# A 2-D DCT kernel: preloaded Sin table, a narrower DCT matrix, float32 loads and halves shared by VectorE and ScalarE

## The chip, the cores and the metric

The kernel runs on one core of a Trainium2 chip. A core has TensorE (matmuls, results in PSUM), VectorE, ScalarE, GpSimd and SyncE, each with its own stream of instructions; they wait for one another through semaphores. The metric is the device time of one execution in microseconds, the median over several runs.

## The reference

For each of 16 images of 64x64 the reference takes the DCT of each row and then of each column:

```python
for k in range(w):            # rows; then the same over columns
    s = 0.0
    for n in range(w):
        s += x[b, i, n] * np.cos(np.pi * k * (2 * n + 1) / (2 * w))
    result[b, i, k] = s
```

With D[n, k] = cos(pi k (2n+1) / 128) this is D^T X D for each image.

## The kernel before

All 16 images are held at once: images 2g and 2g+1 stand on partitions 0 to 63 and 64 to 127, for eight groups g of 64 columns, so that x is a tile of 128 partitions by 512 columns. There is no loop over tiles; the work is one pass with these steps.

*The DCT matrix* (L36 to L94). GpSimd writes the counts k (twice 64 columns) and 2i+1; VectorE forms k(2i+1) + 192, keeps it modulo 256 and turns it into float32 (m_int L55, q_int L65, q_f L74); ScalarE takes Sin of the scaled and shifted value (L80). The modulus is taken because k(2i+1) counts in steps of a 256th of a turn. VectorE clears the two off-diagonal quadrants (L88, L89) and casts to bf16 (L92), which gives DT_2, the 128x128 block-diagonal matrix diag(D, D). In front of the first activation the compiler puts an ACT_TABLE_LOAD, which has the line of that activation.

*The load* (L104). One DMA issued by GpSimd, from float32 in DRAM to bf16 in SBUF.

*The three passes of TensorE.* One matmul with DT_2 over all 512 columns (L107), evicted by VectorE to bf16 (L110); eight transposes against an identity, four for each half of the groups, each half evicted by VectorE (L118, L119); eight matmuls with D (L126), again in halves, each evicted as float32 (L128).

*The store* (L130). One DMA of 256 KB, issued by SyncE when both halves of y_all are there.

The order of an engine's instructions is not that of the code alone: a planner lists them, and gives an engine what it takes to be ready first, the earlier in the code before the later. Each engine then works through its own list in order. Semaphore waits are put in by the framework, by tile and region.

Of the kernel before, what the change touches and what calls it, by code (L numbers as in the profile page):

```python
# [2 lines left out]

# [5 lines left out]


@with_exitstack
def kernel(
    ctx: ExitStack,
    tc: tile.TileContext,
    x: bass.AP,
    out: bass.AP,
):
    nc = tc.nc
    PI = math.pi  # L20

    batch, H, W = x.shape
    assert H == W == 64
    N = H
    P = 128
    G = batch // 2

    f32 = mybir.dt.float32
    bf16 = mybir.dt.bfloat16
    i32 = mybir.dt.int32  # L30

    const = ctx.enter_context(tc.tile_pool(name="const", bufs=1))
    psum = ctx.enter_context(tc.tile_pool(name="psum", bufs=2, space=bass.MemoryType.PSUM))


    iota_k_mod = const.tile([P, P], i32, name="iota_k_mod")  # L36
    nc.gpsimd.iota(iota_k_mod, pattern=[[0, 2], [1, N]], channel_multiplier=0, base=0)  # L37

    iota_2i1 = const.tile([P, 1], i32, name="iota_2i1")
    nc.gpsimd.iota(iota_2i1, pattern=[[0, 1]], channel_multiplier=2, base=1)  # L40

    iota_2i1_int = const.tile([P, 1], i32, name="iota_2i1_int")
    nc.vector.tensor_scalar(  # L43
        iota_2i1_int,
        in0=iota_2i1,
        scalar1=127,
        scalar2=None,
        op0=mybir.AluOpType.bitwise_and,
    )

    iota_2i1_f = const.tile([P, 1], f32, name="iota_2i1_f")
    nc.vector.tensor_copy(iota_2i1_f, iota_2i1_int)  # L52

    m_int = const.tile([P, P], i32, name="m_int")
    nc.vector.tensor_scalar(  # L55
        m_int,
        in0=iota_k_mod,
        scalar1=iota_2i1_f,
        scalar2=192.0,
        op0=mybir.AluOpType.mult,  # L60
        op1=mybir.AluOpType.add,
    )

    q_int = const.tile([P, P], i32, name="q_int")
    nc.vector.tensor_scalar(  # L65
        q_int,
        in0=m_int,
        scalar1=255,
        scalar2=None,
        op0=mybir.AluOpType.bitwise_and,  # L70
    )

    q_f = const.tile([P, P], f32, name="q_f")
    nc.vector.tensor_copy(q_f, q_int)  # L74

    bias_tile = const.tile([P, 1], f32, name="bias_tile")
    nc.gpsimd.memset(bias_tile, -PI)  # L77

    DT_2f = const.tile([P, P], f32, name="DT_2f")
    nc.scalar.activation(  # L80
        DT_2f,
        q_f,
        mybir.ActivationFunctionType.Sin,
        scale=PI / (2.0 * N),
        bias=bias_tile,
    )

    nc.vector.memset(DT_2f[0:N, N:P], 0.0)  # L88
    nc.vector.memset(DT_2f[N:P, 0:N], 0.0)  # L89

    DT_2 = const.tile([P, P], bf16, name="DT_2")
    nc.vector.tensor_copy(DT_2, DT_2f)  # L92

    DT = DT_2[0:N, 0:N]  # L94

    ident_128 = const.tile([P, P], bf16, name="ident_128")
    make_identity(nc, ident_128)


    x_all_hbm = x.rearrange("(g pb) i j -> (pb i) g j", pb=2)  # L100
    out_all_hbm = out.rearrange("(g pb) r c -> (pb r) g c", pb=2)

    x_all = const.tile([P, G, N], bf16, name="x_all")
    nc.gpsimd.dma_start(x_all, x_all_hbm)  # L104

    psum1 = psum.tile([P, G, N], f32, name="psum1", tag="pa")
    nc.tensor.matmul(psum1, DT_2, x_all, start=True, stop=True)  # L107

    t1_all = const.tile([P, G, N], bf16, name="t1_all")
    nc.vector.tensor_copy(t1_all, psum1)  # L110

    HG = G // 2
    t1T_all = const.tile([N, G, P], bf16, name="t1T_all")
    for half in range(2):
        psum2 = psum.tile([N, HG, P], bf16, name=f"psum2_{half}", tag="pb")
        for gi in range(HG):
            g = half * HG + gi
            nc.tensor.transpose(psum2[:, gi, :], t1_all[:, g, :], ident_128)  # L118
        nc.vector.tensor_copy(t1T_all[:, half * HG:(half + 1) * HG, :], psum2)  # L119

    y_all = const.tile([P, G, N], f32, name="y_all")
    for half in range(2):
        psum3 = psum.tile([P, HG, N], f32, name=f"psum3_{half}", tag="pc")
        for gi in range(HG):
            g = half * HG + gi
            nc.tensor.matmul(psum3[:, gi, :], t1T_all[:, g, :], DT,  # L126
                             start=True, stop=True)
        nc.vector.tensor_copy(y_all[:, half * HG:(half + 1) * HG, :], psum3)  # L128

    nc.sync.dma_start(out_all_hbm, y_all)  # L130


# [1 line left out]
_INS = ['x']  # L134
_OUTS = [((16, 64, 64), 'float32')]


# [23 lines left out]
```

## Time and profile before

| | us |
|---|---|
| median of 4 runs | 14.11 (14.11 to 14.12) |
| the profiled execution | 14.11 |
| its span, first to last instruction | 12.3 |
| VectorE busy | 4.3 |
| TensorE matmuls busy | 2.5 |
| GpSimd busy | 2.0 |
| ScalarE busy | 1.7 |

Times in the profile are counted from the start of the span. PE is TensorE's matmuls, PEld its weight loads, DVE VectorE, ACT ScalarE, POOL GpSimd, SP SyncE; a q behind the name is the engine's sequencer. A DMA instruction's own time is only that of issuing it; its data lands later.

### The profile page before, as it was taken

The numbers are of one execution on the slowest core, as the hardware profiler recorded it, in microseconds if no ns is written. First come the engines' busy times: TensorE is split into PE (matmuls) and PEld (weight loads), VectorE is DVE, ScalarE is ACT, GpSimd is POOL, SyncE is SP. The second block draws the span as 40 slices with busy tenths as digits, with TensorE's granted clock in tenths as the row PEclk, the third lists the DMA queues.
The fourth block names the chain that finished last, engine by engine and source line by source line (L and its number), as shares of the span: only waits on it lengthen the run. The fifth ranks groups of instructions, "written<-read, shape, count | busy, mean of one in ns | idle before, by whom it ended". The sixth has DMA issues, their size and how long they took to land.

```text
span 12.3 us, 103 instructions
## 1 busy us (share of the span) xinstructions
PE 2.5 (20%) x17; PEld 1.4 (11%) x17; DVE 4.3 (35%) x13; ACT 1.7 (14%) x2; POOL 2.0 (16%) x10
## 2 busy tenths in 40 slices
PE   0000000000000000089003999789000000000000
PEld 0000000000000000030003993634000000000000
DVE  0001888991000006800794019989950000000000
ACT  0000000005999990000000000000000000000000
POOL 2429799980000000000000000000000000000000
DMA  0000000000899910000000000000000029990000
GB/s 0 0 0 0 0 0 0 0 0 0 54 125 151 85 11 0 0 0 0 0 0 0 0 0 0 0 0 0 0 0 0 0 50 286 289 226 1 0 0 0
DMA packets 2080, 0.39 MB, mean 32 GB/s; under 512 B 2080, under 2 KB 2080, under 8 KB 2080
## 3 DMA queue, kind: packets, MB, share of 16 engines
q0 software_dynamic: 1040, 0.13, 16.7%
q1 hardware_dynamic: 1040, 0.26, 9.4%
HBM read 0.26 MB, written 0.26 MB: 43 GB/s over the span
## 4 chain that ended last, share of the span: by engine, by line
DVE 32%; PE 14%; ACT 10%; issue 6%; ACTq 4%; POOL 3%; POOLq 0%
ACT L80 10%; DVE y_all L128 7%; DVE t_all L110 6%; PE psum L118 5%; PE psum L107 5%; DVE q_int L65 4%; DVE t1T_all L119 3%; ACTq L156 3%; PE psum L126 3%; DVE q_f L74 3%; DVE m_int L55 3%; DVE DT L92 2%; POOL iota_k_mod L37 2%; DVE iota_2i_f L52 1%; DVE iota_2i_int L43 1%
## 5 line engine op out<-in xcount | busy, mean ns | idle before, releaser
L80 ACT ACT_TABLE_LOAD x1 | 1.3, 1283 | 2.9 <-DVE q_f L74 2.9
L107 PE MATMUL psum<-x_all,DT 128*128 128x512 bf16 x1 | 0.6, 606 | 5.3 <-DVE DT L92 5.3
L118 PE MATMUL psum<-ident,t_all 128*64 128x128 bf16 x8 | 1.1, 314 | 0.8 <-DVE t_all L110 0.8
L119 DVE COPY t1T_all<-psum 64x512 bf16<-64x512 bf16 x2 | 0.8, 417 | 0.7 <-PE psum L118 0.7
L104 POOL DMA_DIRECT2D x_all<-in_x_dram x1 | 1.0, 1002 | 0.1
L118 PEld LDWEIGHTS <-t_all 128*64 128x64 bf16 x8 | 0.8, 168 | 1.3 <-DVE t_all L110 1.3
L110 DVE CAST t_all<-psum 128x512 bf16<-128x512 f32 x1 | 0.7, 692 | 0.7 <-PE psum L107 0.7
L128 DVE COPY y_all<-psum 128x256 f32<-128x256 f32 x2 | 0.9, 426 | 0.1
L126 PE MATMUL psum<-DT,t1T_all 64*128 64x64 bf16 x8 | 0.8, 236 | 0.1
L88 DVE MEMSET DT_2f<- 64x64 f32 x1 | 0.1, 112 | 1.8 <-ACT DT_2f L80 1.8
L107 PEld LDWEIGHTS <-DT 128*128 128x128 bf16 x1 | 0.1, 102 | 5.3 <-DVE DT L92 5.3
L43 DVE TENSOR_SCALAR iota_2i_int<-iota_2i 128x1 int32<-128x1 int32 x1 | 0.2, 154 | 1.2 <-POOL bias_tile L77 1.2
L65 DVE TENSOR_SCALAR q_int<-m_int 128x128 int32<-128x128 int32 x1 | 0.5, 521 | 0.0
L126 PEld LDWEIGHTS <-t1T_all 64*128 64x128 bf16 x8 | 0.5, 118 | 0.5 <-DVE t1T_all L119 0.5
L80 ACT ACTIVATE DT_2f<-q_f,bias_tile 128x128 f32<-128x128 f32 x1 | 0.4, 401 | 0.0
L74 DVE CAST q_f<-q_int 128x128 f32<-128x128 int32 x1 | 0.3, 346 | 0.0
L55 DVE TENSOR_SCALAR m_int<-iota_k_mod,iota_2i_f 128x128 int32<-128x128 int32 x1 | 0.3, 319 | 0.0
masks.py:199 POOL TENSOR_SCALAR_AFFINE_SELECT ident<-ident 128x128 bf16<-128x128 bf16 x1 | 0.3, 306 | 0.0
L37 POOL IOTA iota_k_mod<- 128x128 int32 x1 | 0.2, 236 | 0.4 <-POOLq L145 0.4
L92 DVE CAST DT<-DT_2f 128x128 bf16<-128x128 f32 x1 | 0.2, 227 | 0.0
masks.py:197 POOL MEMSET ident<- 128x128 bf16 x1 | 0.2, 201 | 0.0
L52 DVE CAST iota_2i_f<-iota_2i_int 128x1 f32<-128x1 int32 x1 | 0.2, 153 | 0.0
(7 smaller groups left out, 0.7 us busy)
## 6 DMA issues: line engine op xcount, KB each, us to landing
out_dram<-y_all SPq DMA_DIRECT2D x1, 256.0 KB, 2.4
x_all<-in_x_dram POOLq DMA_DIRECT2D x1, 128.0 KB, 3.4
```

The source lines that it names most:

```text
L37: nc.gpsimd.iota(iota_k_mod, pattern=[[0, 2], [1, N]], channel_multiplier=0, base=0)
L55: nc.vector.tensor_scalar(m_int, in0=iota_k_mod, scalar1=iota_2i1_f, scalar2=192.0, op0=mybir.AluOpType.mult, op1=mybir.AluOpType.add,)
L65: nc.vector.tensor_scalar(q_int, in0=m_int, scalar1=255, scalar2=None, op0=mybir.AluOpType.bitwise_and,)
L74: nc.vector.tensor_copy(q_f, q_int)
L80: nc.scalar.activation(DT_2f, q_f, mybir.ActivationFunctionType.Sin, scale=PI / (2.0 * N), bias=bias_tile,)
L104: nc.gpsimd.dma_start(x_all, x_all_hbm)
L107: nc.tensor.matmul(psum1, DT_2, x_all, start=True, stop=True)
L110: nc.vector.tensor_copy(t1_all, psum1)
L118: nc.tensor.transpose(psum2[:, gi, :], t1_all[:, g, :], ident_128)
L119: nc.vector.tensor_copy(t1T_all[:, half * HG:(half + 1) * HG, :], psum2)
L126: nc.tensor.matmul(psum3[:, gi, :], t1T_all[:, g, :], DT, start=True, stop=True)
L128: nc.vector.tensor_copy(y_all[:, half * HG:(half + 1) * HG, :], psum3)
```

## The change

The constants: a dummy activation of Sin on one column is put ahead of everything else; the argument table has 64 columns instead of 128; the count 2i+1 is written separately for the lower and the upper 64 partitions, so that the AND with 127 falls away; Sin writes bf16 at once; the zeroed quadrants and the cast are gone, and DT_wide holds D on partitions 0 to 63 (DT_a) and again on 64 to 127 (DT_b).

The load: two float32 loads, of groups 0 to 3 by SyncE and of groups 4 to 7 by ScalarE, into tiles of their own, and two casts to bf16 on VectorE, which `issue_after` places behind q_f in VectorE's list. A tile of 128 bytes a partition, which nothing uses, is allocated ahead of the two.

The passes: the first matmul becomes four, for each half of the groups one on the lower and one on the upper 64 partitions. Evictions of the first and third pass go to VectorE for half 0 and to ScalarE for half 1; those of the transposes stay on VectorE. The store is issued in halves, by SyncE and by ScalarE.

```diff
@@ -33,101 +33,99 @@
     psum = ctx.enter_context(tc.tile_pool(name="psum", bufs=2, space=bass.MemoryType.PSUM))
 
 
-    iota_k_mod = const.tile([P, P], i32, name="iota_k_mod")
-    nc.gpsimd.iota(iota_k_mod, pattern=[[0, 2], [1, N]], channel_multiplier=0, base=0)
+    dummy = const.tile([P, 1], f32, name="dummy")
+    nc.gpsimd.memset(dummy, 0.0)
+    nc.scalar.activation(dummy, dummy, mybir.ActivationFunctionType.Sin)
 
-    iota_2i1 = const.tile([P, 1], i32, name="iota_2i1")
-    nc.gpsimd.iota(iota_2i1, pattern=[[0, 1]], channel_multiplier=2, base=1)
+    iota_k = const.tile([P, N], i32, name="iota_k")
+    nc.gpsimd.iota(iota_k, pattern=[[1, N]], channel_multiplier=0, base=0)
 
-    iota_2i1_int = const.tile([P, 1], i32, name="iota_2i1_int")
+    iota_2i1m = const.tile([P, 1], i32, name="iota_2i1m")
+    nc.gpsimd.iota(iota_2i1m[0:N, :], pattern=[[0, 1]],
+                   channel_multiplier=2, base=1)
+    nc.gpsimd.iota(iota_2i1m[N:P, :], pattern=[[0, 1]],
+                   channel_multiplier=2, base=1)
+
+    iota_2i1f = const.tile([P, 1], f32, name="iota_2i1f")
+    nc.vector.tensor_copy(iota_2i1f, iota_2i1m)
+
+    m_int = const.tile([P, N], i32, name="m_int")
     nc.vector.tensor_scalar(
-        iota_2i1_int,
-        in0=iota_2i1,
-        scalar1=127,
-        scalar2=None,
+        m_int, in0=iota_k, scalar1=iota_2i1f, scalar2=192.0,
+        op0=mybir.AluOpType.mult, op1=mybir.AluOpType.add,
+    )
+
+    q_int = const.tile([P, N], i32, name="q_int")
+    nc.vector.tensor_scalar(
+        q_int, in0=m_int, scalar1=255, scalar2=None,
         op0=mybir.AluOpType.bitwise_and,
     )
 
-    iota_2i1_f = const.tile([P, 1], f32, name="iota_2i1_f")
-    nc.vector.tensor_copy(iota_2i1_f, iota_2i1_int)
-
-    m_int = const.tile([P, P], i32, name="m_int")
-    nc.vector.tensor_scalar(
-        m_int,
-        in0=iota_k_mod,
-        scalar1=iota_2i1_f,
-        scalar2=192.0,
-        op0=mybir.AluOpType.mult,
-        op1=mybir.AluOpType.add,
-    )
-
-    q_int = const.tile([P, P], i32, name="q_int")
-    nc.vector.tensor_scalar(
-        q_int,
-        in0=m_int,
-        scalar1=255,
-        scalar2=None,
-        op0=mybir.AluOpType.bitwise_and,
-    )
-
-    q_f = const.tile([P, P], f32, name="q_f")
-    nc.vector.tensor_copy(q_f, q_int)
+    q_f = const.tile([P, N], f32, name="q_f")
+    index_done = nc.vector.tensor_copy(q_f, q_int)
 
     bias_tile = const.tile([P, 1], f32, name="bias_tile")
     nc.gpsimd.memset(bias_tile, -PI)
 
-    DT_2f = const.tile([P, P], f32, name="DT_2f")
+    DT_wide = const.tile([P, N], bf16, name="DT_wide")
     nc.scalar.activation(
-        DT_2f,
-        q_f,
-        mybir.ActivationFunctionType.Sin,
-        scale=PI / (2.0 * N),
-        bias=bias_tile,
+        DT_wide, q_f, mybir.ActivationFunctionType.Sin,
+        scale=PI / (2.0 * N), bias=bias_tile,
     )
 
-    nc.vector.memset(DT_2f[0:N, N:P], 0.0)
-    nc.vector.memset(DT_2f[N:P, 0:N], 0.0)
-
-    DT_2 = const.tile([P, P], bf16, name="DT_2")
-    nc.vector.tensor_copy(DT_2, DT_2f)
-
-    DT = DT_2[0:N, 0:N]
+    DT_a = DT_wide[0:N, :]
+    DT_b = DT_wide[N:P, :]
 
     ident_128 = const.tile([P, P], bf16, name="ident_128")
     make_identity(nc, ident_128)
 
-
+    HG = G // 2
     x_all_hbm = x.rearrange("(g pb) i j -> (pb i) g j", pb=2)
     out_all_hbm = out.rearrange("(g pb) r c -> (pb r) g c", pb=2)
 
+    pad = const.tile([P, 32], f32, name="pad")   # 128 bytes, never used
+    x_all_f0 = const.tile([P, HG, N], f32, name="x_all_f0")
+    x_all_f1 = const.tile([P, HG, N], f32, name="x_all_f1")
+    nc.sync.dma_start(x_all_f0, x_all_hbm[:, 0:HG, :])
+    nc.scalar.dma_start(x_all_f1, x_all_hbm[:, HG:G, :])
+
     x_all = const.tile([P, G, N], bf16, name="x_all")
-    nc.gpsimd.dma_start(x_all, x_all_hbm)
-
-    psum1 = psum.tile([P, G, N], f32, name="psum1", tag="pa")
-    nc.tensor.matmul(psum1, DT_2, x_all, start=True, stop=True)
+    with tc.issue_after(index_done.ins):
+        nc.vector.tensor_copy(x_all[:, 0:HG, :], x_all_f0)
+        nc.vector.tensor_copy(x_all[:, HG:G, :], x_all_f1)
 
     t1_all = const.tile([P, G, N], bf16, name="t1_all")
-    nc.vector.tensor_copy(t1_all, psum1)
+    t1T_all = const.tile([N, G, P], bf16, name="t1T_all")
+    y_all = const.tile([P, G, N], f32, name="y_all")
+    out_engines = [nc.sync, nc.scalar]
 
-    HG = G // 2
-    t1T_all = const.tile([N, G, P], bf16, name="t1T_all")
+    def evict(half, out_, in_):
+        # VectorE takes half 0, ScalarE half 1
+        if half == 0:
+            nc.vector.tensor_copy(out_, in_)
+        else:
+            nc.scalar.copy(out_, in_)
+
     for half in range(2):
+        hs = slice(half * HG, (half + 1) * HG)
+        psum1 = psum.tile([P, HG, N], f32, name=f"psum1_{half}", tag="pa")
+        nc.tensor.matmul(psum1[0:N, :, :], DT_a, x_all[0:N, hs, :], start=True, stop=True)
+        nc.tensor.matmul(psum1[N:P, :, :], DT_b, x_all[N:P, hs, :], start=True, stop=True)
+        evict(half, t1_all[:, hs, :], psum1)
+    for half in range(2):
+        hs = slice(half * HG, (half + 1) * HG)
         psum2 = psum.tile([N, HG, P], bf16, name=f"psum2_{half}", tag="pb")
         for gi in range(HG):
-            g = half * HG + gi
-            nc.tensor.transpose(psum2[:, gi, :], t1_all[:, g, :], ident_128)
-        nc.vector.tensor_copy(t1T_all[:, half * HG:(half + 1) * HG, :], psum2)
-
-    y_all = const.tile([P, G, N], f32, name="y_all")
+            nc.tensor.transpose(psum2[:, gi, :], t1_all[:, half * HG + gi, :], ident_128)
+        nc.vector.tensor_copy(t1T_all[:, hs, :], psum2)
     for half in range(2):
+        hs = slice(half * HG, (half + 1) * HG)
         psum3 = psum.tile([P, HG, N], f32, name=f"psum3_{half}", tag="pc")
         for gi in range(HG):
-            g = half * HG + gi
-            nc.tensor.matmul(psum3[:, gi, :], t1T_all[:, g, :], DT,
+            nc.tensor.matmul(psum3[:, gi, :], t1T_all[:, half * HG + gi, :], DT_a,
                              start=True, stop=True)
-        nc.vector.tensor_copy(y_all[:, half * HG:(half + 1) * HG, :], psum3)
-
-    nc.sync.dma_start(out_all_hbm, y_all)
+        evict(half, y_all[:, hs, :], psum3)
+        out_engines[half].dma_start(out_all_hbm[:, hs, :], y_all[:, hs, :])
 
 
 # ---- launch: one core; inputs and outputs as the reference has them ----
```

## Rows read from the trace of the kernel before

**Rows 1.** The page's first part: the span, and busy time, share and instructions of each engine.

```profile
span 12.3 us, 103 instructions
PE 2.5 (20%) x17; PEld 1.4 (11%) x17; DVE 4.3 (35%) x13; ACT 1.7 (14%) x2; POOL 2.0 (16%) x10
```

**Rows 2.** The chain of waits, in order of time: start us, us, what.

```profile
0.75 0.01 POOLq L37
...
2.48 0.36 DVE q_f L74
...
2.91 1.28 ACT L80
4.19 0.42 ACTq L156
...
4.67 0.11 DVE DT_2f L88
...
4.98 0.24 DVE DT L92
...
5.27 0.62 PE psum L107
...
5.91 0.70 DVE t_all L110
...
6.66 0.65 PE psum L118 x4
...
7.33 0.43 DVE t1T_all L119
...
7.80 0.41 PE psum L126 x4
...
8.23 0.85 DVE y_all L128 x2
```

**Rows 3.** DMA issues: line, KB each, us from issue to landing.

```profile
out_dram<-y_all SPq DMA_DIRECT2D x1, 256.0 KB, 2.4
x_all<-in_x_dram POOLq DMA_DIRECT2D x1, 128.0 KB, 3.4
```

**Rows 4.** The timeline of GpSimd: start us, us, instruction [idle before].

```profile
1.03 0.13 POOL L40 IOTA iota_2i<- 128x1 int32 x1
1.10 0.10 POOL L77 MEMSET bias_tile<- 128x1 f32 x1
...
1.42 1.00 POOL L104 DMA_DIRECT2D x_all<-in_x_dram  x1
2.43 0.31 POOL masks.py:199 TENSOR_SCALAR_AFFINE_SELECT ident<-ident 128x128 bf16<-128x128 bf16 x1
```

**Rows 5.** Groups of instructions by form: line, shapes, count | busy us, mean ns | idle before.

```profile
L118 PE MATMUL psum<-ident,t_all 128*64 128x128 bf16 x8 | 1.1, 314 | 0.8 <-DVE t_all L110 0.8
L128 DVE COPY y_all<-psum 128x256 f32<-128x256 f32 x2 | 0.9, 426 | 0.1
L107 PE MATMUL psum<-x_all,DT 128*128 128x512 bf16 x1 | 0.6, 606 | 5.3 <-DVE DT L92 5.3
L65 DVE TENSOR_SCALAR q_int<-m_int 128x128 int32<-128x128 int32 x1 | 0.5, 521 | 0.0
L80 ACT ACTIVATE DT_2f<-q_f,bias_tile 128x128 f32<-128x128 f32 x1 | 0.4, 401 | 0.0
L55 DVE TENSOR_SCALAR m_int<-iota_k_mod,iota_2i_f 128x128 int32<-128x128 int32 x1 | 0.3, 319 | 0.0
L92 DVE CAST DT<-DT_2f 128x128 bf16<-128x128 f32 x1 | 0.2, 227 | 0.0
L52 DVE CAST iota_2i_f<-iota_2i_int 128x1 f32<-128x1 int32 x1 | 0.2, 153 | 0.0
```

**Rows 6.** The timeline of the transposes and of SyncE's store: start us, us, instruction.

```profile
6.66 1.06 PE L118 MATMUL psum<-ident,t_all 128*64 128x128 bf16 x8 [0.78 <-DVE t_all L110]
...
9.11 0.40 SPq L130 DMA_DIRECT2D out_dram<-y_all  x1
```

**Rows 7.** Stretches of the span: busy time of each engine, PEclk, DMA share, GB/s.

```profile
3.20:4.60 1.40, 0.00 (x0) 0.00 (x0) 0.00 (x0) 1.39 (x2) 0.00 (x0) 1.00 1.44 92
...
10.10:11.15 1.05, 0.00 (x0) 0.00 (x0) 0.00 (x0) 0.00 (x0) 0.00 (x0) 1.00 1.08 245
```

More of the change, by code (lines that the diff above doesn't have):

```diff
@@ L6 @@
 import concourse.tile as tile
-from concourse import bass_utils, mybir
+from concourse import mybir
 from concourse.masks import make_identity
```

## The prediction, made before the changed kernel had run

> **What bounds the kernel now.** I read the totals first [rows 1]: no engine is busy for more than 35% of the 12.3 us span, so nothing is limited by throughput; the kernel is one chain of hand-overs, and only what lies on that chain has a price. So the chain of waits comes next [rows 2]. The reader is to see three stretches in it. From 0.75 to 5.22 us the DCT matrix is built: GpSimd counts, VectorE makes an argument table (the last of it is q_f, done at 2.84), ScalarE loads its Sin table for 1.28 us and evaluates Sin until 4.6, VectorE clears two quadrants and casts. From 5.27 to 9.08 us the data passes through TensorE and the evictions of PSUM. From 9.11 the output is stored: 2.4 us to landing [rows 3], then 0.8 us of closing barriers to the span's end at 12.3. The profiled execution took 14.11 us, which is also the median of the four runs shown; 1.8 us of it lie outside the span, and I leave these 1.8 and the 0.8 as they are.
>
> What is not on the chain is x: its load is issued by GpSimd at 1.42 [rows 4] and takes 3.4 us to landing [rows 3], so it is there at 4.8, 0.4 us ahead of the DCT matrix. That 0.4 is the first thing to see: shortening the matrix alone would win no more than 0.4 us, so the new load counts as much as the table.
>
> **The change, part by part**, in us from the span's start.
>
> *Matrix.* The DCT argument table becomes 64 columns wide instead of 128, one of the four small VectorE steps goes (the AND on iota_2i1), and so do the two MEMSETs and the cast behind Sin (4.67 to 5.22). GpSimd does a tiny memset more ahead of its iota and one more short iota; rows of this size follow each other by some 0.07 us [rows 4], and the iota of 64 columns is shorter, so the index column is ready at about 1.25 where it was at 1.16. Then four VectorE steps: one at 128x1 took 0.153, those at 128x128 from 0.32 to 0.52 beside a working GpSimd and the plain cast 0.227 [rows 5]; at 64 columns I take 0.22 with the hand-over each, at most 0.35. q_f is done at 2.1 (2.6 at most).
>
> *Table load.* The first activation is now a dummy that depends only on a memset, so the 1.283 us load no longer waits for q_f. ScalarE also issues half of the load of x. On GpSimd the load of x ran ahead of the affine select that stands before it in the code and was not ready [rows 4], so this planner issues what is ready first; I expect the same on ScalarE, at the body's start at 0.75, with 0.40 us for the issue, as SP's row has it [rows 6]. Then the table load 1.15 to 2.43, the dummy to at most 2.83 and Sin to at most 3.23, each put at the 0.401 that the 128-wide Sin took [rows 5]. The matrix is ready by 3.25 without any step of VectorE behind it.
>
> The Trainium skill speaks against this price ("ScalarE: Activation LUTs", What ACT_TABLE_LOAD costs): each switch of table is put at some 1.28 us of load and 1.38 us of drain, 2.66 in all. Here the load begins at 2.91 and the row behind it, where Sin runs, at 4.19 [rows 2], so this trace shows nothing between them and does not agree with the page. By the page's figure the matrix would come 1.38 later, at 4.6 instead of 3.25; what that would do is rival 4.
>
> *Load of x.* One GpSimd load with a cast in flight becomes two float32 loads of 128 KB, issued by SP and ScalarE at about 0.75, with two casts on VectorE. The bytes into SBUF double to 256 KB. The nearest row is the store: 256 KB in the same 256-byte pieces, issued by SP, 2.4 us to landing; it moved 245 GB/s in the 1.05 us in which it ran fully [rows 7]. I take 2.4 for both halves together, since both run on the same DMA engines: landing at 3.15. The bounds are 1.9 (half the bytes) and 3.4, the row of GpSimd's load [rows 3]. The price of a cast: 0.153 at one column and 0.227 at 128 give 0.30 at 256 [rows 5]; 0.43 if it runs at the pace of the 256-column eviction. Cast 0 runs from 3.2 to 3.5, cast 1 from 3.53 to 3.83. So x is now what the first matmul waits for, by a quarter of a us: 3.55 instead of 5.27, a gain of 1.72. What hides the matrix is x; if x came half a us earlier, only 0.25 of it would be won.
>
> *First matmul.* One of 128 rows and 512 columns becomes two pairs of 64 rows and 256 columns. The one took 0.606 [rows 5]; eight transposes of 128 columns, 0.314 each, take 1.06 together [rows 5, 6], so they begin 0.106 apart, so a column costs 0.83 ns and 0.18 is fixed. A pair in series costs the same 0.61 and ends at 4.16; the second pair follows at once to 4.59. The eviction of half 0 takes 0.43 on VectorE, as y_all's rows at the same shape: 4.20 to 4.63. Before, matmul and eviction filled 5.27 to 6.61, that is 1.34; now 1.08: a gain of 0.26.
>
> *ScalarE's copies.* The trace has no PSUM copy on ScalarE. The nearest rows: 0.401 for its 128-wide Sin, 0.426 for VectorE's copy of this shape [rows 5]. I take 0.43, with 0.40 and 0.80 (twice the Sin's columns at twice its time) as the ends. Half 1 is evicted from 4.63 to 5.06, while the transposes of half 0 run (4.68 to 5.33, four in 0.65 as before [rows 2]), so 0.27 of slack covers it; at 0.80 the last 0.1 would show.
>
> *From there* the order is as before: copies of t1T to 5.78 and 6.21 (0.43 each), matmuls of half 1 from 6.26 to 6.67, then y half 1, now on ScalarE, to 7.12, issue at 7.15. VectorE finishes y half 0 at 6.68 and SP issues it at 6.71. From the first transpose to the last issue the trace has 2.45 (6.66 to 9.11) and my sum 2.47: ScalarE's second copy only stands where VectorE's stood, since the matmuls of half 1 end just when VectorE would be free. ScalarE at 0.80 would cost 0.37 here, with nothing to hide it.
>
> *Store.* Half 0 goes out 0.44 earlier, so its packets are almost through when half 1's start. A store of 256 KB spends about 1.06 of its 2.4 in packets [rows 7]; half of the bytes leave 1.87: landing at 9.02 instead of 11.5, of which 0.53 is the gain of the split. If two queues cost as much as one whole store, that 0.53 is gone.
>
> Sum: 1.72 + 0.26 − 0.02 + 0.53 = 2.49; 14.11 − 2.49 = 11.62, told as **11.6 us**.
>
> **The rivals.**
>
> 1. *The pair of matmuls runs side by side*: they use different rows and columns of the array, so the second need not wait for the first's columns. For it: different partitions on both sides; against: every row here shows matmuls in a queue, one after another. A pair then costs 0.18 + 0.21 = 0.39 in place of 0.61: 11.4 us. The Trainium skill has this rule ("TensorEngine Tiling (Array Packing)", Key Properties): tiles of the array work independently of each other. No run here shows it yet.
>
> 2. *ScalarE's load goes behind Sin.* If the planner keeps the code's order, half 1 of x is issued at 3.23 and lands at 5.1 (1.87 later, as half of a store). Cast 1 stands on VectorE ahead of the eviction of half 0, and half 1's matmuls on TensorE ahead of all transposes, so both halves wait: cast to 5.45, matmuls to 6.1, transposes from 6.1 instead of 4.68: 1.42 later, 13.0 us. Against it: GpSimd's order [rows 4].
>
> 3. *The dummy doesn't move the table load*: it is loaded behind q_f still, or a second time for Copy ahead of Sin. Then the load runs from 2.12 to 3.40, the matrix is ready at 3.8, 0.3 behind x: 11.9 us.
>
> 4. *ScalarE stands still behind the early load*, for about as long as the load itself takes, 1.28: the dummy begins at 3.71 and not at 2.43, the matrix is ready at 4.53, the first matmul begins at 4.58, 1.03 later: 12.65 us. The chain speaks against it: 4.19 follows 2.91 by the load's 1.28 and nothing more [rows 2]. The drain that the Trainium skill states on the page named above is this case.
>
> 5. *Slower than before.* No row shows a DMA from ScalarE. The queue of waiters in rival 2 has a point from which it decides: half 1 of x may land at 3.8 for nothing, and beyond that each us late is a us of the whole, because VectorE and TensorE work in order; from 6.3 on the kernel is slower than 14.11. That needs the issue behind Sin (3.23) and a landing as slow as GpSimd's 3.4: 6.63, which gives 14.4 us. For it: only that ScalarE's queue is unmeasured. Against it: both halves of the condition.
>
> **How the numbers follow.** My forecast 0.59, rival 1 0.23, rival 2 0.06, rival 3 0.05, rival 4 0.03, rival 5 0.03, and 0.01 that gains and losses cancel. The forecast alone with its unknown prices: ScalarE's copies (+0.5 at worst), the load (−0.25, where the matrix takes over, to +0.3, where its packets run for the 1.4 of GpSimd's load [rows 7]), casts (+0.13): 11.3 to 12.2. Rival 1 reaches below that, to 11.0 if x also comes early and the dummy and Sin are shorter than 0.4. The range is 11.0 to 12.2, which takes in rival 3 and leaves out rivals 2, 4 and 5. Faster by over 0.2% (0.03 us, about what can be told from no change): all but rival 5 and the cancelling case, 0.96; the same 0.01; slower 0.03.
>
> **What would show it.** The table load should begin before 1.2 and no second one appear; the two loads be issued before 0.9 and land near 3.15; the first matmul wait for VectorE's cast and not for Sin; two matmuls of a pair begin 0.21 apart (together, in rival 1); ScalarE's copies take about 0.43; the last issue stand near 7.15 and its landing under 1.9 behind it. I am wrong if the first matmul waits for ScalarE, if half 1 of x is issued behind Sin, or if the last landing is still 2.4 behind its issue.

## The result, and the profile after

The changed kernel takes 11.36 us in the median of 11 runs (11.23 to 11.55); the kernel before took 14.11 in 15 runs (14.10 to 14.12). The ratio is 0.799, with a 95% interval from 0.797 to 0.801. The forecast was 11.6 in a range from 11.0 to 12.2. This ratio and those below are of the fast runs alone, those within 1.5% of the fastest of their kernel, while the medians are of all runs (11.36 to 14.11 is 0.805). The profiled execution took 11.50 us with a span of 9.72, and times worked out from its trace are to be compared with 11.50.

The page's first part for the changed kernel:

```profile
span 9.7 us, 114 instructions
## 1 busy us (share of the span) xinstructions
PE 2.5 (26%) x20; PEld 1.7 (17%) x20; DVE 3.1 (31%) x10; ACT 2.5 (25%) x5; POOL 1.2 (13%) x11
```

No engine is near its limit here either. TensorE is as busy as before [rows 1]; VectorE has lost 1.2 us, and ScalarE has gained 0.8. The chain of waits (start us, us, what) shows where the time is now:

```profile
0.74 2.52 DMA x_all_f<-in_x_dram
...
3.28 0.30 DVE x_all L94
...
3.62 0.37 PE psum L112
3.99 0.07 PE psum L113
...
4.08 0.43 DVE t_all L105
...
4.56 0.65 PE psum L119 x4
...
5.23 0.43 DVE t1T_all L120
...
5.70 0.39 PE psum L125 x4
...
6.13 0.41 PE psum L125 x4
...
6.56 0.37 ACT y_all L107
```

Read it against the chain of before [rows 2]. The whole first stretch, with q_f, the table load, Sin, MEMSETs and a cast, has left the chain; one DMA and one cast stand in its place, and the first matmul begins at 3.62 instead of 5.27. The matrix is not on the chain at all. The timeline of ScalarE and TensorE (start us, us, instruction, idle before) says how early it is:

```profile
1.27 1.28 ACT L38 ACT_TABLE_LOAD   x1 [1.27 <-PEq L143]
...
2.56 0.20 ACT L38 ACTIVATE dummy<-dummy 128x1 f32<-128x1 f32 x1
2.67 0.33 ACT L71 ACTIVATE DT_wide<-q_f,bias_tile 128x64 bf16<-128x64 f32 x1
3.05 0.12 PEld L112 LDWEIGHTS <-DT_wide 64*64 64x64 bf16 x1 [3.05 <-ACT DT_wide L71]
...
3.62 0.37 PE L112 MATMUL psum<-x_all,DT_wide 64*64 64x256 bf16 x1 [3.62 <-DVE x_all L94]
...
3.63 0.42 PE L113 MATMUL psum<-x_all,DT_wide 64*64 64x256 bf16 x1
...
4.35 0.37 ACT L107 CAST t_all<-psum 128x256 bf16<-128x256 f32 x1 [1.35 <-PE psum L113]
```

The weights are loaded at 3.05, and the matmul waits 0.57 longer, for the cast of x. The two matmuls of the pair begin together. The DMA issues (KB each, us from issue to landing):

```profile
x_all_f<-in_x_dram SPq DMA_DIRECT2D x1, 128.0 KB, 2.5
x_all_f<-in_x_dram ACTq DMA_DIRECT2D x1, 128.0 KB, 2.8
out_dram<-y_all SPq DMA_DIRECT2D x1, 128.0 KB, 1.9
out_dram<-y_all ACTq DMA_DIRECT2D x1, 128.0 KB, 2.0
```

The last issue stands at 6.96, before at 9.11 [rows 6], and the last landing at 8.92 instead of 11.46.

### The profile page after: what moved, and what is told of

It is laid out like the page before. It is cut to its first block, busy times and chain, and to the rows that moved or that the text cites. A ratio compares the mean times of both kernels' runs of the same rounds, so it can differ in the third digit from the quotient of the medians.

```text
span 9.7 us, 114 instructions
## 1 busy us (share of the span) xinstructions
PE 2.5 (26%) x20; PEld 1.7 (17%) x20; DVE 3.1 (31%) x10; ACT 2.5 (25%) x5; POOL 1.2 (13%) x11
## 4 chain that ended last, share of the span: by engine, by line
DMA 26%; PE 19%; DVE 12%; ACT 4%; issue 3%
DMA x_all_f<-in_x_dram 26%; PE psum L125 8%; PE psum L119 7%; DVE t_all L105 4%; DVE t1T_all L120 4%; ACT y_all L107 4%; PE psum L112 4%; DVE x_all L94 3%; PE psum L113 1%
## 5 line engine op out<-in xcount | busy, mean ns | idle before, releaser
L112 PE MATMUL psum<-x_all,DT_wide 64*64 64x256 bf16 x2 | 0.6, 368 | 3.6 <-DVE x_all L94 3.6
L125 PE MATMUL psum<-DT_wide,t1T_all 64*128 64x64 bf16 x8 | 0.8, 236 | 0.1
L113 PE MATMUL psum<-x_all,DT_wide 64*64 64x256 bf16 x2 | 0.7, 418 | 0.0
L94 DVE CAST x_all<-x_all_f 128x256 bf16<-128x256 f32 x1 | 0.3, 293 | 1.0 <-DMA x_all_f<-in_x_dram 1.0
L105 DVE COPY y_all<-psum 128x256 f32<-128x256 f32 x1 | 0.4, 426 | 0.1
L95 DVE CAST x_all<-x_all_f 128x256 bf16<-128x256 f32 x1 | 0.3, 295 | 0.0
```

What stands on the lines that cost most here:

```text
L94: nc.vector.tensor_copy(x_all[:, 0:HG, :], x_all_f0)
L95: nc.vector.tensor_copy(x_all[:, HG:G, :], x_all_f1)
L105: nc.vector.tensor_copy(out_, in_)
L112: nc.tensor.matmul(psum1[0:N, :, :], DT_a, x_all[0:N, hs, :], start=True, stop=True)
L113: nc.tensor.matmul(psum1[N:P, :, :], DT_b, x_all[N:P, hs, :], start=True, stop=True)
L125: nc.tensor.matmul(psum3[:, gi, :], t1T_all[:, half * HG + gi, :], DT_a, start=True, stop=True)
```

## The experiments

Twelve kernels were run, each beside the kernel before (14.11 or 14.12 every time), but in three groups on different chips and not beside the changed kernel. A difference of medians from the changed kernel is therefore weaker than one of stretches in two traces.

| run | median us (lowest to highest) | ratio to before, 95% |
|---|---|---|
| table_only | 14.07 (13.98 to 14.20) | 0.993 to 0.999 |
| load_only | 13.58 (13.58 to 13.59) | 0.960 to 0.964 |
| load_behind_sin | 13.14 (13.01 to 13.16) | 0.924 to 0.934 |
| loads_on_sp | 11.58 (11.40 to 11.91) | 0.806 to 0.815 |
| gpsimd_dma_added | 14.10 (14.09 to 14.11) | 0.998 to 1.000 |
| no_dummy | 12.17 (12.15 to 12.44) | 0.860 to 0.864 |
| same_rows | 11.59 (11.42 to 11.69) | 0.809 to 0.816 |
| no_cast | 11.37 (11.22 to 11.46) | 0.794 to 0.806 |
| no_pad | 11.97 (11.88 to 11.99) | 0.844 to 0.849 |
| table_only_aligned | 13.83 (13.73 to 13.93) | 0.975 to 0.985 |
| one_store | 12.03 (12.00 to 12.07) | 0.851 to 0.854 |
| sp_loads_no_cast | 11.22 (11.05 to 11.60) | 0.785 to 0.790 |

**One part of the change alone: table_only and load_only.** The first is the kernel before plus

```diff
+    dummy = const.tile([P, 1], f32, name="dummy")
+    nc.gpsimd.memset(dummy, 0.0)
+    nc.scalar.activation(dummy, dummy, mybir.ActivationFunctionType.Sin)
```

> The kernel before with the dummy activation alone. My theory (matrix and load of x are two parallel paths that end 0.4 us apart): the matrix is ready near 4.0, but x still lands at 4.8, so the first matmul starts at 4.85 instead of 5.27 and the time is 13.7 us. Rival (one chain, each part worth its own length): the whole 1.28 us of the table load is won, 12.8 us.

Measured: 14.07. The matrix was ready at 4.0, as expected, and the first matmul waited for x until 4.98, 0.29 earlier than before. In the chain of waits:

```profile
1.43 3.51 DMA x_all<-in_x_dram
...
4.98 0.60 PE psum L111
```

But the store took 2.61 us from issue to landing instead of 2.35, and gave 0.26 of it back. Both theories missed that; it is taken up below. The DMA issue:

```profile
out_dram<-y_all SPq DMA_DIRECT2D x1, 256.0 KB, 2.6
```

The second kernel of this pair is the kernel before with

```diff
 ...
+    nc.sync.dma_start(x_all_f0, x_all_hbm[:, 0:HG, :])
+    nc.scalar.dma_start(x_all_f1, x_all_hbm[:, HG:G, :])
 ...
-    nc.gpsimd.dma_start(x_all, x_all_hbm)
+    with tc.issue_after(index_done.ins):
+        nc.vector.tensor_copy(x_all[:, 0:HG, :], x_all_f0)
+        nc.vector.tensor_copy(x_all[:, HG:G, :], x_all_f1)
```

> The kernel before with the two float32 loads and the two casts alone; the table load still stands behind q_f. My theory: x is in bf16 by 3.9, the matrix still comes at 5.22, and VectorE has the casts done before Sin ends, so the time stays 14.1 us (within 0.1). Rival (the load is what the change lives on): 12.5 us or less.

Measured: 13.58, so my theory fell: a load that was off the chain was worth 0.53. The matrix itself came earlier, and with it the first matmul, at 4.82 instead of 5.27. To see whether GpSimd's issuing of the load had slowed VectorE, that issue was put back into load_only, with a destination that nothing reads:

```diff
+    x_unused = const.tile([P, G, N], bf16, name="x_unused")
+    nc.gpsimd.dma_start(x_unused, x_all_hbm)
```

> The load-only kernel (e2) with GpSimd issuing its old load again, into a tile that nothing reads. The load-only kernel was 0.53 us faster than the kernel before although the table load stayed where it was; in its trace the AND (q_int) took 0.23 us where it took 0.52, the cast q_f 0.23 for 0.35, and q_f was done at 2.37 for 2.84. Theory A (GpSimd's 1.0 us of issuing slows the VectorE instructions beside it): q_int goes back to 0.5, q_f ends near 2.85, the time back to 14.0 to 14.1 us. Theory B (the load itself came off the path): VectorE's steps stay at 0.23 and the time at 13.6 us.

Measured: 14.10, theory A. The groups by form (busy us, mean ns) of load_only:

```profile
L55 DVE TENSOR_SCALAR m_int<-iota_k_mod,iota_2i_f 128x128 int32<-128x128 int32 x1 | 0.3, 288 | 0.0
...
L65 DVE TENSOR_SCALAR q_int<-m_int 128x128 int32<-128x128 int32 x1 | 0.2, 227 | 0.0
L74 DVE CAST q_f<-q_int 128x128 f32<-128x128 int32 x1 | 0.2, 227 | 0.0
```

and with GpSimd's DMA added:

```profile
L65 DVE TENSOR_SCALAR q_int<-m_int 128x128 int32<-128x128 int32 x1 | 0.5, 522 | 0.0
...
L74 DVE CAST q_f<-q_int 128x128 f32<-128x128 int32 x1 | 0.3, 347 | 0.0
...
L55 DVE TENSOR_SCALAR m_int<-iota_k_mod,iota_2i_f 128x128 int32<-128x128 int32 x1 | 0.3, 306 | 0.0
```

The same instruction takes 227 ns with GpSimd idle and 522 beside its DMA issue, and q_f ends at 2.82 instead of 2.37. The load's traffic is not the cause, for its packets begin at 3.1 only, behind q_f. So the old load cost nothing by its landing and 0.45 us by the engine that issued it. It does not slow every step alike: m_int, beside the same issue, took 306 ns instead of 288, and q_f's 347 fall beside the affine select, which the issue had pushed back from 1.40 to 2.42. The Trainium skill ("SBUF — State Buffer", Who interferes with whom) has a port pair that GpSimd shares with VectorE's copies, casts and tensor_scalars when these run in a fast mode; the later one waits. That q_int, begun behind the issue, lost 295 ns agrees with that in direction; no run here shows the port itself, and a wait to the issue's end at 2.40 would have put q_int's end at 2.63, where it stands at 2.43.

**The start address of a tile: no_pad and table_only_aligned.** In table_only and, further below, in no_dummy the store was slow. In both, a small tile had come or gone ahead of y_all in the partition. No trace gives a tile's address: the offsets here are counted from the tiles' sizes in order of allocation, a small tile taken as 32 bytes.

```diff
-    pad = const.tile([P, 32], f32, name="pad")   # 128 bytes, never used
```

> The changed kernel without the unused tile of 128 bytes. Two runs so far had a store slower than all others: table_only (packets 1.30 us for 256 KB, elsewhere 1.05) and no_dummy (0.75 for 128 KB, elsewhere 0.59). In both, a tile put in or left out ahead of y_all made it start 32 and 224 bytes past a multiple of 256 bytes of a partition; in all the others it starts on one. Without the unused tile it starts 128 bytes past. Theory A (a 256-byte row that straddles such a multiple costs more): packets of a half 0.75, last landing 2.2 behind its issue instead of 1.95, the loads slower as well, 11.6 to 11.9 us. Theory B (the unused tile does nothing): 11.36.

Measured: 11.97, 0.61 above the changed kernel and somewhat above theory A's range. The store's stretch (us, busy time by engine, PEclk, DMA share, GB/s) of the changed kernel:

```profile
7.50:8.60 1.10, 0.00 (x0) 0.00 (x0) 0.00 (x0) 0.00 (x0) 0.00 (x0) 1.00 1.06 238
```

and without the unused tile:

```profile
7.65:9.00 1.35, 0.00 (x0) 0.00 (x0) 0.00 (x0) 0.00 (x0) 0.00 (x0) 1.00 0.87 194
```

The same 256 KB take a quarter longer, and the last half of the store lands 2.19 behind its issue instead of 1.95. The unused tile in the change is therefore no ornament. But these 0.24 are all that the trace puts down to it. Of the 0.41 between the profiled executions (11.91 and 11.50) the other 0.17 comes with x: half 0 lands at 3.42 instead of 3.25, and with aligned tiles it landed anywhere from 3.17 (same_rows) to 3.46 (no_cast). That the loads are slower as well, as theory A has it, is therefore not shown. The Trainium skill ("DMA: Bandwidth & Descriptors", How a descriptor splits into AXI transactions) says that a descriptor which does not start on a 256-byte boundary is split into more transactions, the first of them from the boundary below; the store agrees with that in direction. Then the same repair for table_only:

```diff
+    pad = const.tile([P, 56], f32, name="pad")   # 224 bytes, never used
```

> table_only with an unused tile of 224 bytes ahead of x_all, so that x_all and y_all start on multiples of 256 bytes again. Theory A (table_only lost its gain to the store's start): the store takes 2.35 from issue to landing instead of 2.61, the load lands at 4.8 to 4.9, the first matmul starts at 4.85 to 4.95, 13.7 to 13.8 us. Theory B (the gain was lost elsewhere): 14.05 us as before.

Measured: 13.83 (13.73 to 13.93), against 14.07: theory A. The store's stretch in table_only, 256 KB at 201 GB/s:

```profile
9.75:11.05 1.30, 0.00 (x0) 0.00 (x0) 0.00 (x0) 0.00 (x0) 0.00 (x0) 1.00 0.76 201
```

and aligned:

```profile
9.70:10.75 1.05, 0.00 (x0) 0.00 (x0) 0.00 (x0) 0.00 (x0) 0.00 (x0) 1.00 1.10 249
```

**The dummy taken away: no_dummy.** The three lines of the first diff are left out of the changed kernel.

> The changed kernel without the dummy activation, so that the table load waits for q_f: rival 3 made real. My theory (matrix and x are parallel paths, x the later by some 0.5 us): q_f at 2.25, table load to 3.55, Sin to 3.9, first matmul at 4.0 instead of 3.62: 0.4 us slower than the changed kernel, 11.75 us. Rival (the dummy is worth its whole table load): 12.6 us. Rival (x hides it all): 11.36.

Measured: 12.17. On TensorE the theory held: the first matmul begins at 3.99, expected at 4.0, and its wait has changed its name, in the timeline,

```profile
3.99 0.42 PE L108 MATMUL psum<-x_all,DT_wide 64*64 64x256 bf16 x1 [3.99 <-ACT DT_wide L67]
```

and the last issue is 0.37 later. Against the profiled execution of the changed kernel the whole is 0.66 longer (12.16 and 11.50); 0.26 more of it is the store: without the dummy's 32 bytes y_all starts 224 past a multiple of 256, and the last half lands 2.21 behind its issue instead of 1.95.

**A late half: load_behind_sin and loads_on_sp.**

```diff
 ...
+    with tc.issue_after(sin_done.ins):
         nc.scalar.dma_start(x_all_f1, x_all_hbm[:, HG:G, :])
```

> The changed kernel with ScalarE's half of the load placed behind Sin in ScalarE's list: rival 2 of the prediction made real. By that rival's words both halves wait for the late one, and the time is 13.0 us less what the measured kernel is under the forecast, 12.8. But the planner's list for this kernel puts all of half 0's transposes and last matmuls ahead of half 1's first matmul and the second cast behind the copy of t1T, so I expect: half 0 as early as a load alone allows (first matmul at 3.0), half 1 one pass later, last issue near 8.2 instead of 6.96: 12.6 us. If a late half cost nothing: 11.4.

Measured: 13.14. The planner did reorder, as its timeline shows: half 1's cast (L96) and first matmul stand behind half 0's transposes.

```profile
3.41 0.37 PE L113 MATMUL psum<-x_all,DT_wide 64*64 64x256 bf16 x1 [3.41 <-DVE x_all L95]
...
5.36 0.28 DVE L96 CAST x_all<-x_all_f 128x256 bf16<-128x256 f32 x1
...
5.82 0.42 PE L113 MATMUL psum<-x_all,DT_wide 64*64 64x256 bf16 x1
```

So rival 2 had the time nearly right (13.0), by luck, and the way wrong: half 1 was there at 4.52 and waited for engines, because the planner had put it last. Most of what my 12.6 lacked is half 0's landing, 3.04 instead of 2.65. The next run asks what half 0 gains if half 1 does not share its time:

```diff
-    nc.scalar.dma_start(x_all_f1, x_all_hbm[:, HG:G, :])
+    nc.sync.dma_start(x_all_f1, x_all_hbm[:, HG:G, :])
```

> The changed kernel with both halves of the load issued by SP, half 0 first. My theory (the two queues share the same DMA engines, and packets of both halves interleave, so that half 0 lands as late as both): half 0 lands near 2.65 instead of 3.25, ScalarE's table load starts 0.5 earlier, the matrix is ready at 2.7, the first matmul starts at 3.0 instead of 3.62, half 1 lands by 3.3 and is covered by half 0's work: 10.75 us. Rival (issuing costs more than sharing: half 1 issued 0.43 later makes all 0.4 later): 11.7 us. Third: the issuer does not matter, 11.3 to 11.4.

Measured: 11.58 (11.40 to 11.91), not 10.75. Half 0, now ahead of half 1 in one queue, lands 2.29 behind its issue, not 1.9, and half 1 at 3.88, 2.66 behind its own. The timeline of VectorE, TensorE and ScalarE:

```profile
3.40 0.37 PE L112 MATMUL psum<-x_all,DT_wide 64*64 64x256 bf16 x1 [3.40 <-DVE x_all L94]
...
3.91 0.29 DVE L95 CAST x_all<-x_all_f 128x256 bf16<-128x256 f32 x1 [0.56 <-DMA x_all_f<-in_x_dram]
4.12 0.42 DVE L105 CAST t_all<-psum 128x256 bf16<-128x256 f32 x1
4.25 0.37 PE L112 MATMUL psum<-x_all,DT_wide 64*64 64x256 bf16 x1 [0.44 <-DVE x_all L95]
...
4.71 0.37 ACT L107 CAST t_all<-psum 128x256 bf16<-128x256 f32 x1 [2.02 <-PE psum L113]
```

The first matmul is 0.22 earlier and its result ready by 3.83, but VectorE stands in front of the second cast until 3.88, with the eviction behind it: it begins at 4.12 instead of 4.08. This is the queue of waiters of rivals 2 and 5; it costs half 0 some 0.25. Yet it is not what set the time. The chain that ended last runs from half 1's landing through its cast, its matmuls at 4.25 and ScalarE's eviction at 4.71 (4.35 in the changed kernel) to its transposes, and the last issue stands at 7.11 instead of 6.96.

**The pair of matmuls: same_rows.**

```diff
-        nc.tensor.matmul(psum1[N:P, :, :], DT_b, x_all[N:P, hs, :], start=True, stop=True)
+        nc.tensor.matmul(psum1[N:P, :, :], DT_a, x_all[0:N, hs, :], start=True, stop=True)
```

> The changed kernel with the second matmul of each pair reading the lower 64 partitions too (the second half of the images is left out of the result): same columns and same work, but both matmuls on the same rows of the array. Theory A (a pair runs side by side only where both its rows and its columns differ): the second begins 0.21 behind the first, the pair takes 0.61 instead of 0.42, the time 11.55 us. Theory B (different columns are enough): they still begin together, 11.36 us.

Measured: 11.59 (11.42 to 11.69), which overlaps the changed kernel's spread and decides nothing; the trace does, for theory B:

```profile
3.54 0.37 PE L112 MATMUL psum<-x_all,DT_wide 64*64 64x256 bf16 x1 [3.54 <-DVE x_all L94]
...
3.54 0.42 PE L113 MATMUL psum<-x_all,DT_wide 64*64 64x256 bf16 x1
```

The two begin together on the same rows of the array too, and VectorE's eviction of the pair begins 0.46 behind them in both kernels (4.00 after 3.54, 4.08 after 3.62). Different columns are enough.

**The casts: no_cast and sp_loads_no_cast.**

```diff
-        nc.vector.tensor_copy(x_all[:, 0:HG, :], x_all_f0)
-        nc.vector.tensor_copy(x_all[:, HG:G, :], x_all_f1)
+    x_hi = [t.bitcast(bf16).rearrange("p g (n two) -> p g n two", two=2)
+            for t in (x_all_f0, x_all_f1)]
 ...
```

> The changed kernel without the two casts: TensorE reads the upper 16 bits of each float32 of x as bf16, every second element of the tile, so x is cut to bf16 instead of rounded. My theory (x's landing and cast set the first matmul): it begins right behind the landing, at 3.3 instead of 3.62, and the time is 11.03 us. Rival (reading every second element slows the matmul): the pair takes 0.85 instead of 0.42 and eats the gain, 11.4 us or more. Rival (the matrix takes over): first matmul at 3.1 or later in any case, so at most 0.5 is won.

Measured: 11.37 (11.22 to 11.46): no gain in the median. The matmul runs at its old pace (0.37 and 0.42) and begins 0.04 behind the landing, but in this execution the landing came at 3.46; fifteen of the sixteen parts of the load were there by 3.16. Why the fastest of the four executions was not below 11.22 either is open, and so is what the casts are worth.

The next run joins these edits to that of loads_on_sp:

```diff
-    nc.scalar.dma_start(x_all_f1, x_all_hbm[:, HG:G, :])
+    nc.sync.dma_start(x_all_f1, x_all_hbm[:, HG:G, :])
 ...
```

> Both loads on SP, half 0 first (as loads_on_sp), and no casts (as no_cast, x cut to bf16). In loads_on_sp half 0 was ready 0.2 earlier, but VectorE stood behind the late half's cast, so the eviction of half 0 began no earlier; without casts this wait is gone. Theory A: first matmul at 3.07, eviction of half 0 by 3.95, half 1 lands at 3.6 to 3.9, transposes of half 0 from 4.1 to 4.35 instead of 4.56, 10.9 to 11.15 us. Theory B (a late half 1 holds TensorE, whose half-1 matmuls stand ahead of the transposes): transposes not before 4.4, 11.25 us or more.

Measured: 11.22 (11.05 to 11.60), between the theories. Transposes begin at 4.25, the time of theory A, but by the way of theory B: half 0's eviction ends at 3.99, and half 1's matmuls, which stand ahead on TensorE, hold the transposes back. Half 1 lands at 3.85 and now leads the chain,

```profile
1.22 2.63 DMA x_all_f<-in_x_dram
...
3.90 0.37 PE psum L110
```

with a wait of its eviction between the two halves of the transposes. The kernel's interval against before (0.785 to 0.790) is below that of the changed kernel (0.797 to 0.801), about 1% faster. But the two were not run beside each other, their spreads overlap, and x is cut instead of rounded.

**The split of the store: one_store.**

```diff
-        out_engines[half].dma_start(out_all_hbm[:, hs, :], y_all[:, hs, :])
+    nc.sync.dma_start(out_all_hbm, y_all)
```

> The changed kernel with one store of 256 KB on SP behind both halves of y. My theory (half 0's packets run while half 1 is still computed): issued at 6.96 it lands 2.35 later instead of 1.95, so 0.4 us slower than the changed kernel, 11.75 us; the prediction had put this term at 0.53. Rival (two stores share the DMA engines and cost as much as one): 11.36.

Measured: 12.03. From the last issue to the landing the single store takes 2.33, the second half of the split one 1.95: 0.38 of the 0.40 expected. The DMA issue:

```profile
out_dram<-y_all SPq DMA_DIRECT2D x1, 256.0 KB, 2.3
```

In the profiled executions (12.00 and 11.50) another 0.09 is a later first matmul, at 3.71. The medians differ by 0.67. The four executions of one_store lie within 12.00 to 12.07, so x presumably came late in all of them; why it did is open.

## Why the forecast came out as it did

*What bounds the kernel, and what follows the table load: right.* Matrix and x are two paths, and x became the later one. The first matmul began at 3.62, forecast 3.55. The two paths miss each other by 0.57, where I had 0.3: the table load began 0.12 late, behind an issue of ScalarE of 0.49 instead of 0.40, but the dummy took 0.20 and Sin 0.33 instead of 0.4 each. That shortening the matrix alone wins at most 0.4 held: 0.28 with aligned tiles. That it is the load that must come along held as well, though load_only showed a second reason, which the prediction did not have: the load's issue on GpSimd had lengthened the matrix's own path by 0.45.

*Load of x: the size was off.* From the store I took 1.9 for one half and 2.4 for both; a half alone lands 2.30 behind its issue (load_behind_sin), both at 2.52 and 2.78. That half 1 came 0.37 behind the forecast, at 3.52 instead of 3.15, cost nothing by luck: its cast stands behind half 0's on VectorE and began at 3.55, forecast 3.53. The cast took 0.29, as worked out.

*First matmul: the step that failed.* "A pair in series" was the likeliest case; the pair runs side by side, rival 1. From first matmul to first transpose it is 0.94 where I had 1.13. Before it was 1.39; no run separates what the pair and what the halving gave of that step. The Trainium skill's rule that stood beside rival 1 ("TensorEngine Tiling (Array Packing)", Key Properties) agrees with the trace.

*ScalarE's copies*: 0.372, not 0.43, and below the bound of 0.40 that I had put under them. From first transpose to last issue 2.40, forecast 2.47.

*Store*: the last half lands 1.95 behind its issue, forecast 1.87.

*No stand-still behind the table load* (rival 4): the dummy begins at 2.56, the load ends at 2.55. The drain of 1.38 us that the Trainium skill states ("ScalarE: Activation LUTs", What ACT_TABLE_LOAD costs) is not there in this kernel, whose only table load is its first.

*What no step priced*: the unused tile. It does nothing by itself, but without it the store takes 0.24 longer, and so much of the forecast's 2.49 would have been gone. The kernel without it took 11.97, 0.61 more than the changed one; the rest goes with a later x, which is not shown to be the tile's doing.

The terms together, against the profiled execution: +0.07 for the first matmul, −0.19 for the pair and its eviction, −0.07 for the copies and what lies behind them, +0.08 for the landing, −0.02 for the rest: 11.62 becomes 11.49, measured 11.50. So part of the nearness is that a load and a landing 0.15 dearer stand against a pair and copies 0.26 cheaper. What is left to the median of 11.36 is, as far as the traces show, the load. In three kernels that are alike from the first matmul on, time less start of that matmul is the same (changed: 11.50 − 3.62; same_rows: 11.42 − 3.54; no_cast: 11.39 − 3.50; 7.88, 7.88, 7.89), so the spread of 11.23 to 11.55 is presumably that of x's landing; one execution of each has a trace. The kernel before hid its load, and its runs lie within 0.02.

## What to carry to other kernels

Where a chain has two paths that end 0.4 us apart, neither alone is worth much: 0.28 for the one, 0.53 for the other (and that for a side effect). With both, and a narrower matrix, the first matmul begins 1.65 earlier, and the whole change is worth 2.75. Before pricing a DMA by its landing, look at what its issuing engine does to the instructions beside it. And when a small tile is added or removed, look at where the tiles behind it start: here 32 bytes were worth 0.26 us on a store.

## What the runs showed of the hardware

- A store of 256-byte rows is slower by a quarter where its tile does not start on a multiple of 256 bytes in the partition, as counted: 1.30 instead of 1.05 us of packets for 256 KB (32 bytes off), 0.76 (224 bytes off) and 0.76 to 0.79 (128 off) instead of 0.60 for 128 KB. For loads no run shows it.
- A VectorE instruction of 227 ns (q_int) took 522 beside a DMA issue of GpSimd, another of 288 (m_int) 306.
- Two matmuls that write different halves of PSUM's partitions begin within 10 ns of each other, with the same or different rows: 0.42 us for the pair, where one of double the columns took 0.61 [rows 5].
- TensorE reads every second bf16 of a tile at the pace of adjoining ones: 0.37 us for 256 columns and 0.46 from its begin to the eviction's either way.
- A load of 128 KB in 256-byte rows took 2.2 to 2.3 us to landing alone, a store of the same form 1.9 (load_behind_sin).
